# Two hybrid decoder layers in one kernel: FFN gate summed beside the output projection and closed as rows, upward product's last operand split one product sooner, closing work of the FFN spread out

## Chip, core, metric

One core of one Trainium2 chip. The metric is device time in microseconds (us); lower is better. The kernel before took 1864.57 us, the median of 3 runs (1862.85 to 1871.15).

## What is computed

Two layers over x of 1024 positions and 1024 channels, float32. Cut to what matters here:

```python
mod = silu(c) @ ada_w[l] + ada_b[l]                 # 6 rows of 1024: shift, scale, gate, twice
h = rms_norm(x, g_pre_mix[l]) * (1 + scale_m) + shift_m
q, k, v, u = split(h @ w_in[l] + b_in[l])           # 512, 128, 128, 512 columns
mix = concat([sliding_window_attention(q, k, v), causal_pool_mixer(u)]) @ w_out[l]
x = x + gate_m * rms_norm(mix, g_post_mix[l])
h = rms_norm(x, g_pre_ffn[l]) * (1 + scale_f) + shift_f
f = (silu(h @ w_gate[l]) * (h @ w_up[l])) @ w_down[l]     # 2816 channels between
x = x + gate_f * rms_norm(f, g_post_ffn[l])
```

The last `gate_f` is what this page calls the FFN gate: a row of 1024 numbers, made from the vector c and a 1024 x 1024 block of ada_w alone.

## The kernel before

Every large product is made of three matmuls in a rounded format: each operand is split into a rounded part `hi` and a remainder `lo` (`split`, L221: ScalarE rounds at L223, VectorE subtracts at L224), and hi·hi + hi·lo + lo·hi are summed in a PSUM bank (`mm3`; `mm` issues at L286). There are four `acc` banks, three `msc` banks and one `pv` bank, each 128 x 512. The sequence is worked on in two halves of 512 positions, four tiles of 128 each.

A layer goes through these stages:

1. Input projection, attention and pooling of both halves, and the output projection of each half (`mix_out`, `natural_proj`). On TensorE the order is written out by hand: `weave` runs a main stream and takes steps of side chains (attention, pooling, sums for the modulation) as soon as enough matmul columns have been issued. The unit of their gaps is `STEP`, twelve matmuls of 512 columns. `LEADS`, `GAPS`, `CLOSE` and the numbers in the calls are such gaps.
2. The upward product (w_gate and w_up together), by a seven-product scheme (Strassen-like) over 2 x 2 blocks. `up_firsts` makes the two products that need only the first half; `up_pair` makes the other five for each of 11 pairs of channel blocks. A product is two banks of four steps of three matmuls, so 24 matmuls.
3. The downward product (`down`), by the same scheme: p1, p2, p5, p6, p3, p7, p4, each over 11 pairs.

Outside the hand-written part the order of instructions on an engine is set when the program is built; engines run their own queue strictly in that order. SyncE ("SP") issues nearly all DMAs in the same way.

In `up_pair` (L1350) two `raw` buffers of 128 x 2048 hold a pair's weights: `raws[0]` has a11 and a21, `raws[1]` has a12 and a22. There are only two such buffers, so the next pair's loads (L1358) wait until the last split or sum has read the old ones. The products are, in order, T2 (a21+a22-a11, sums L1390 and L1391), T3 (a22-a11, L1396), T1 (a21+a22), B22 (a12 less the first sum, L1395) and T4 (a22 itself). `times` splits a product's left operand into `hi` and `lo`, of which there are three tiles of 1024 each, and multiplies. `added` evicts a bank with VectorE (L1375). `gated` applies silu on ScalarE (L1300) and multiplies on VectorE (L1301). L1409, L1411, L1413 and L1420 form sums that the downward product needs; `keep` stores (L1378).

The modulation rows are summed on VectorE: `ada_sum` and `ada_flow` multiply the eight 128 x 512 pieces of a block by a number per partition and accumulate (L367 and L369 in the one, L611 and L613 in the other). The sum over partitions is then a matmul with ones. `ada_gate_columns` closes a gate with four 128x1 products a half (L562), and turns the columns into rows with a transpose (L575); `ada_gate` closes it with two products whose result is one row of 512 columns (L543, L544). The FFN gate is summed by `ada_stream` during the upward product and closed as columns. The next layer's rows are summed during the downward product of layer 0 (42 steps asked of them in 77).

In `natural_proj` the last step k evicts: for each of four banks three matmuls, a square sum on ScalarE, and a multiplication by G on VectorE (L850). The second half of the columns needs the same banks again. `post_ffn` and `finish` add the residual (L769, L770); `ended` does what follows a closed bank in `down` (evictions L1470).

Of the kernel before, what the change touches and what calls it, by code (L numbers as in the profile page):

```python
# [12 lines left out]
F32R = mybir.dt.float32r  # L13
# [55 lines left out]
def hybrid_decoder_kernel(  # L69
# [556 lines left out]
    CLOSE = 1.35  # L626
# [145 lines left out]
    def post_ffn(h, fn, ss, G, into=None):  # L772
# [3 lines left out]
        sq = t_("rs", [P, 8])  # L776
        for t in range(NT):
# [7 lines left out]
            nc.sync.dma_start(new[rows, :], fn[t])  # L785
            yield
        spill[h] = new
        normalise(fn, inv_rms(sq), into)
        yield
# [31 lines left out]
    def natural_proj(fn, left, wsrc, ss, G, last, free):  # L821
# [7 lines left out]
        for nh in range(2):  # L829
# [3 lines left out]
            for k in range(K):  # L833
# [7 lines left out]
                else:  # L841
# [3 lines left out]
                    split(lh, ll, left[k])  # L845
                for t in range(NT):
                    mm3(banks[t], lh[:, tiles[t]], ll[:, tiles[t]], wh, wl, k == 0, k == K - 1)
                    if k == K - 1:
                        square_sum(ss, t, nh, banks[t])
                        nc.vector.tensor_mul(fn[t][:, cs], banks[t], G[:, cs])  # L850
                    yield
# [316 lines left out]
    LEADS = (0.9, 0.9, 0.25, 2.72, 1.2, 0.64)  # L1168
# [181 lines left out]
    def up_pair(l, p, ops, kept, xs):  # L1350
# [55 lines left out]
        bank = times(a12, B22)  # L1406
        added(X, bank, X)
# [8 lines left out]
        bank = times(a22, T4)  # L1416
# [24 lines left out]
    def left_of(a, p0, p1, c0, c1):  # L1441

        n, w = p1 - p0, c1 - c0
        raw, lh, ll = (
            part(tag, 2 * w).rearrange("p (i n) -> p i n", n=w)[:, :n, :] for tag in ("raw", "hi", "lo")
        )
        nc.sync.dma_start(raw, a[:, p0:p1, c0:c1])
        split(lh, ll, raw)
        return lh, ll
# [8 lines left out]
    def down(l, wd, load, kept, fn, ended, last, prelude):  # L1458
# [91 lines left out]
        for ts in ((0, 1), (2, 3)) if last else (range(NT),):  # L1550
            banks = {t: acc_bank() for t in ts}
            final = []
            for g, (p0, p1) in enumerate(DOWN_GROUPS):
                n = p1 - p0
                lh, ll = left_of(kept[a], p0, p1, ts[0] * P, (ts[-1] + 1) * P)
# [103 lines left out]
    FIRST = (3, NPAIR - 3)  # L1659
    for l in range(DEPTH):  # L1660
# [29 lines left out]
        def gate_flow():  # L1690
            if l:
                return
            one, two = ada_gate(l, 0)
            yield from ada_flow([one], [cats[0][1][:, i, :] for i in range(4)], 2.99)
            while 1 not in cats:
                yield 0.5
            yield from ada_flow([two], [cats[1][1][:, i, :] for i in range(4)], 2.12)
# [19 lines left out]
        pair = Chain(ada_flow(ada_pair(l, 1, par["cols"], par["abf"]), ring, 0.91))  # L1717
# [6 lines left out]
        def first_half():  # L1724
            for _ in post_norm(0, fn, ss, res0):
                yield 0.58
# [36 lines left out]
        weave(dense1(), att, pair, pre, pool)  # L1763
# [3 lines left out]
        weave(out1, att)  # L1767
# [3 lines left out]
        def second_norm():  # L1771
            yield from post_norm(1, fn, ss, xs)
            region("up")
# [8 lines left out]

        norm = second_norm()
        run(firsts[1], 16 * FIRST[1], (norm, NT + 2 + HK + 2))
        drain(norm)

        nxt, jobs = None, []
        if l + 1 < DEPTH:
            nxt = layer_cols(l + 1)
# [3 lines left out]
        wd, load = down_loads(l)  # L1793

        def ups():
            for p in range(NPAIR):
                for i, _ in enumerate(up_pair(l, p, ops, kept, firsts_x if p < sum(FIRST) else None)):
# [3 lines left out]
                    yield  # L1801

        run(ups(), 5 * NPAIR + 2 * (NPAIR - sum(FIRST)), (side, 2 * ADA + 4))
        drain(side)
        G = load_gate(l, 1)
        side = ada_stream(jobs)
# [6 lines left out]
        tail, aheads, ready = [], [], []  # L1813

        def ended(name, t):
# [22 lines left out]
        def between():  # L1838
# [10 lines left out]
            yield from post_ffn(0, fn[0], ss[0], G)  # L1849
# [6 lines left out]
            (between(), 7 * NPAIR), (side, 42),  # L1856
        )
        if nxt:
            region("mix")
            xs1 = wide_tiles("cfb")  # L1860
            drain(post_ffn(1, fn[1], ss[1], G, xs1))
# [37 lines left out]
```

## Time and profile before

| | |
|---|---|
| median of 3 runs | 1864.57 us |
| profiled execution | 1868.22 us |
| its span, first to last instruction | 1866.5 us |
| mean granted clock of TensorE | 0.996 |
| first matmul starts | 12 us after the span's start |
| output projection of the second half | about 286 to 330 us, and 1205 to 1249 us |
| upward product, five products a pair | about 418 to 732 us, and 1337 to 1648 us |

Of a row of the profile: the engine (PE is TensorE's matmuls, PEld its weight loads, DVE is VectorE, ACT is ScalarE, SP is SyncE), the line of the kernel, the operation, what it writes and reads (`lo<-raw,hi`), shape and type, and how many. In a timeline the first two numbers are start and length in us, and brackets hold the engine's idle time before it and who ended it. Matmuls overlap: a matmul of 512 columns is shown with 0.39 us, but in a dense row they start 0.227 us apart.

### The profile page before, as it was taken

Reading aid. Unit: us, or ns where it says so; the run is one execution under the profiler, and the core shown is the slowest. Engines: PE = TensorE matmul, PEld = TensorE weight load, DVE = VectorE, ACT = ScalarE, POOL = GpSimd, SP = SyncE. Lnnn points to the kernel's source line nnn. Section 1 sums busy time; section 2 is a strip of 40 time slices with the busy share of each in tenths; the row PEclk is TensorE's granted clock in tenths of the full one; section 3 lists DMA queues with packets and bytes.
Section 4 is the critical chain, followed back from the end, with each engine's and each line's share of the span. In section 5 each row is a group of like instructions: output and inputs, shape, how many; then the busy total and the mean of one; then the engine's idle time right before and its main releaser. Section 6 shows DMA issues by size and latency. Waiting matters only on the chain.

```text
span 1866.5 us, 25197 instructions
## 1 busy us (share of the span) xinstructions
PE 1826.6 (98%) x8641; PEld 1509.6 (81%) x8641; DVE 1493.2 (80%) x2468; ACT 928.1 (50%) x1770; POOL 75.3 (4%) x144
## 2 busy tenths in 40 slices
PE   7999999999999999999999999999999999999998
PEld 5887888888788788888888878888887887888886
DVE  7799885688878878799967798856888887877687
ACT  4885895562222223454657758856522222244452
POOL 0022110000000000000001201100000000000000
PEclk9999999999999999999999999999999999999999
DMA  9637654665555465955577475546646555574343
GB/s 323 233 118 231 241 167 142 215 216 174 170 182 186 173 223 188 318 187 177 196 254 240 147 237 212 172 145 214 217 151 204 176 191 204 190 267 142 116 141 119
DMA packets 237166, 363.84 MB, mean 195 GB/s; under 512 B 17951, under 2 KB 126439, under 8 KB 237037
## 3 DMA queue, kind: packets, MB, share of 16 engines
q1 hardware_dynamic: 236428, 360.12, 57.6%
q10 hardware_dynamic: 576, 2.10, 0.3%
q8 instruction: 68, 1.11, 0.2%
q14 instruction: 62, 0.50, 0.1%
q0 software_dynamic: 32, 0.00, 0.0%
HBM read 274.58 MB, written 87.57 MB: 194 GB/s over the span
## 4 chain that ended last, share of the span: by engine, by line
PE 69%; DVE 15%; DMA 7%; ACT 5%; issue 3%; SPq 1%; DVEq 0%; ACTq 0%; POOL 0%; POOLq 0%
PE acc L286 63%; DVE lo L224 3%; PE msc L286 3%; PE msc L291 2%; DMA raw<-in_w_up_dram 2%; DMA raw<-in_w_gate_dram 1%; DMA ar<-x 1%; DVE fn L1375 1%; ACT hi L223 1%; PE pv L286 1%; DVE ada L613 1%; ACT sb L1076 1%; DVE raw L1390 1%; DVE raw L1391 1%; DVE fn L1301 1%
## 5 line engine op out<-in xcount | busy, mean ns | idle before, releaser
L223 ACT ACTIVATE hi<-raw 128x1024 fp32r<-128x1024 f32 (+2 forms) x360 | 315.2, 887 | 371.5 <-PE acc L286 238.6
L224 DVE TENSOR_TENSOR lo<-raw,hi 128x1024 fp32r<-128x1024 f32 (+2 forms) x360 | 362.6, 1013 | 111.9 <-ACT hi L223 111.3
L286 PE MATMUL acc<-t,hi 128*128 128x512 f32 x1408 | 437.8, 393 | 7.9 <-ACT hi L223 7.9
L286 PEld LDWEIGHTS acc<-t,hi 128*128 128x128 f32 x1408 | 265.8, 189 | 65.0 <-ACT hi L223 9.9
L286 PE MATMUL acc<-hT,hi 128*128 128x512 f32 x928 | 287.2, 395 | 0.0
L286 PE MATMUL acc<-t,lo 128*128 128x512 f32 x704 | 275.1, 392 | 0.4 <-DVE lo L224 0.3
L286 PE MATMUL acc<-bh,hi 128*128 128x512 f32 x520 | 203.1, 391 | 0.6 <-DVE sb L1470 0.6
L286 PE MATMUL acc<-bh,lo 128*128 128x512 f32 x520 | 202.5, 390 | 0.0
L286 PEld LDWEIGHTS acc<-hT,hi 128*128 128x128 f32 x928 | 168.6, 188 | 31.1
L286 PE MATMUL acc<-hT,lo 128*128 128x512 f32 x512 | 188.1, 391 | 0.0
L1375 DVE TENSOR_TENSOR fn<-acc,fn 128x512 f32<-128x512 f32 x220 | 150.3, 684 | 36.8 <-PE acc L286 36.3
L286 PEld LDWEIGHTS acc<-t,lo 128*128 128x128 f32 x704 | 133.0, 189 | 30.0 <-DVE lo L224 1.7
L286 PE MATMUL acc<-ph,hi 128*128 128x512 f32 x328 | 126.6, 390 | 0.0
L1300 ACT ACTIVATE fn<-fn 128x512 f32<-128x512 f32 x44 | 27.9, 633 | 196.2 <-DVE fn L1375 196.2
L286 PEld LDWEIGHTS acc<-bh,hi 128*128 128x128 f32 x520 | 97.6, 188 | 21.3 <-DVE sb L1470 1.1
L286 PEld LDWEIGHTS acc<-bh,lo 128*128 128x128 f32 x520 | 97.6, 188 | 20.4
L286 PEld LDWEIGHTS acc<-hT,lo 128*128 128x128 f32 x512 | 95.5, 188 | 20.4
L286 PE MATMUL acc<-hi,hT 128*128 128x512 f32 (+1 forms) x416 | 109.1, 349 | 1.4 <-ACT hT L223 0.7
L286 PE MATMUL acc<-b,hi 128*128 128x512 f32 x352 | 108.3, 389 | 0.0
L223 ACT ACTIVATE bh<-two_b 128x512 fp32r<-128x512 f32 x100 | 62.3, 623 | 72.0 <-PE acc L286 66.7
L286 PE MATMUL acc<-hi 128*128 128x512 f32 x224 | 88.3, 394 | 2.5 <-DVE fn L850 2.4
L286 PE MATMUL acc<-lo,hi 128*128 128x512 f32 x224 | 87.3, 390 | 0.0
(327 smaller groups left out, 3171.4 us busy)
## 6 DMA issues: line engine op xcount, KB each, us to landing
raw<-in_w_gate_dram SPq DMA_DIRECT2D x44, 512.0 KB, 3.9
raw<-in_w_up_dram SPq DMA_DIRECT2D x44, 512.0 KB, 5.4
ar<-in_ada_w_dram SPq DMA_DIRECT2D x80, 256.0 KB, 3.5
raw<-keeps SPq DMA_DIRECT2D x40, 512.0 KB, 4.6
cfb<-in_ada_w_dram SPq DMA_DIRECT2D x72, 256.0 KB, 3.2
keeps<-fn SPq DMA_DIRECT2D x66, 256.0 KB, 2.1
two_b<-in_w_down_dram SPq DMA_DIRECT2D x30, 512.0 KB, 5.8
raw<-in_w_in_dram SPq DMA_DIRECT2D x52, 256.0 KB, 4.2
```

The source lines that it names most:

```text
L223: a = nc.scalar.activation(hi, src, AF.Copy)
L224: v = nc.vector.tensor_sub(lo, src, hi.bitcast(F32))
L286: return nc.tensor.matmul(dst, lhs, rhs, start=start, stop=stop)
L291: return nc.tensor.transpose(dst, src, eye_)
L613: ins = nc.vector.scalar_tensor_tensor(acc, w, c_, acc, op0=ALU.mult, op1=ALU.add)
L1076: nc.scalar.activation(S[:, i, :], S[:, i, :], AF.Exp, bias=nm[:, i : i + 1], accum_out=sm[:, i : i + 1])
L1300: nc.scalar.activation(g, g, AF.Silu)
L1301: nc.vector.tensor_mul(dst, g, u)
L1375: nc.vector.tensor_add(halves_of(dst)[m], bank, halves_of(src)[m])
L1390: nc.vector.tensor_add(a21, a21, a22)
L1391: nc.vector.tensor_sub(a11, a21, a11)
```

## The change

- The FFN gate of both layers is summed by `ada_flow` beside the second half's output projection, with two `ar` tiles as its ring (gap 1.9 STEP), and closed as rows by `ada_gate`. During layer 0's upward product the next layer's rows are summed instead, one step (two accumulations) a pair at the fourth product; during layer 1's, nothing. In the downward product 27 steps are asked instead of 42.
- `up_pair` splits a22 into two `hT` tiles of its own (`mine`), in the program text one product sooner.
- `natural_proj` holds its last step but one back and runs the last two steps bank by bank.
- The next layer's columns are read right after the second half's norm instead of after the upward product's first part.
- `post_ffn` takes two steps of the stream for one, and stores of the second half are put off. `gate_right`, the scaling by G at the end of p7 in layer 1, is put off by 4, 6, 14 and 16 steps. In the last product of layer 1 the second pass's first two left operands get `bh` tiles.
- Gaps: CLOSE 1.35 to 1.59, the second of LEADS 0.9 to 0.85, the gate's flow 2.99 to 2.54 and 2.12 to 2.11, the pair's 0.91 to 0.86, `first_half` 0.58 to 0.61.

```diff
+            if into:
+                held.append([t + 1, nc.sync.dma_start, new[rows, :], fn[t]])
...
+    held = held + [(k, lh, ll, wh, wl)] if k > K - 2 else [(k, lh, ll, wh, wl)]
+    if k == K - 2:
+        continue
     for t in range(NT):
-        mm3(banks[t], lh[:, tiles[t]], ll[:, tiles[t]], wh, wl, k == 0, k == K - 1)
-        if k == K - 1:
-            square_sum(ss, t, nh, banks[t])
-            nc.vector.tensor_mul(fn[t][:, cs], banks[t], G[:, cs])
-        yield
+        for kk, lh, ll, wh, wl in held:
+            mm3(banks[t], lh[:, tiles[t]], ll[:, tiles[t]], wh, wl, kk == 0, kk == K - 1)
+            if kk == K - 1:
+                square_sum(ss, t, nh, banks[t])
+                nc.vector.tensor_mul(fn[t][:, cs], banks[t], G[:, cs])
+            yield
...
+        def parted(src, hi, lo):
+            split(*(d.rearrange("p (a b) -> p a b", b=P) for d in (hi, lo)), src)
+            return hi, lo
         def times(src, right):
-            hi, lo = part("hi", 1024), part("lo", 1024)
-            split(*(d.rearrange("p (a b) -> p a b", b=P) for d in (hi, lo)), src)
-            return double(hi, lo, ops[right])
+            return double(*parted(src, part("hi", 1024), part("lo", 1024)), ops[right])
...
         bank = times(a12, B22)
+        parted(a22, *mine)
...
-        bank = times(a22, T4)
+        bank = double(*mine, ops[T4])
...
+        def ffn_gate():
+            yield from ada_flow(ada_gate(l, 1), [t_("ar", [P, 512]) for _ in range(2)], GATE_GAP)
...
-        weave(out1, att)
+        turn_.due = issued[0] + GATE_BEGIN * STEP
+        weave(out1, att, turn_)
+        finish_off(turn_)
...
-        side = ada_stream(ada_gate_columns(l, 1, par["cols"]))
+        side = ada_stream(jobs)
...
+                    if i == SUM_STEP and p < NPAIR - 1:
+                        next(side, None)
-        run(ups(), 5 * NPAIR + 2 * (NPAIR - sum(FIRST)), (side, 2 * ADA + 4))
+        run(ups())
...
-                    nc.vector.tensor_mul(ready[t][:, 512:D], fn[1][t][:, 512:D], G[:, 512:D])
+                    pending.append([4 + 2 * t + 6 * (t // 2), gate_right, t])
```

Lines below the edits have other numbers after the change: L1301 is L1312, L1375 is L1388, L1390 is L1403, L1391 is L1404, L1395 is L1408, L1396 is L1409, L1409 is L1423, L1411 is L1425, L1413 is L1427, L1420 is L1434, and L850 is L861.

VectorE in the upward product of layer 1, from the remainder of a pair's first left operand (`lo`) on. Before, at a pair with two steps of the gate (`ada`):

```order
L224 TENSOR_TENSOR lo<-raw,hi 128x1024
L1301 TENSOR_TENSOR fn<-fn 128x512
L1375 TENSOR_TENSOR fn<-acc,fn 128x512
L1409 TENSOR_TENSOR sb<-fn,sb 128x512
L369 SCALAR_TENSOR_TENSOR ada<-ar,c_act,ada 128x512
L1411 TENSOR_TENSOR fn<-sb,sa 128x512
L1413 TENSOR_TENSOR fn<-sa,fn 128x512
L1375 TENSOR_TENSOR fn<-acc,fn 128x512
L369 SCALAR_TENSOR_TENSOR ada<-ar,c_act,ada 128x512
L1301 TENSOR_TENSOR fn<-fn 128x512
L1396 TENSOR_TENSOR raw<-raw 128x8x128
```

The same place now:

```order
L224 TENSOR_TENSOR lo<-raw,hi 128x1024
L1409 TENSOR_TENSOR raw<-raw 128x8x128
L1388 TENSOR_TENSOR fn<-acc,fn 128x512
L1312 TENSOR_TENSOR fn<-fn 128x512
L224 TENSOR_TENSOR lo<-raw,hi 128x1024
L1423 TENSOR_TENSOR sb<-fn,sb 128x512
L1388 TENSOR_TENSOR fn<-acc,fn 128x512
L1425 TENSOR_TENSOR fn<-sb,sa 128x512
L1427 TENSOR_TENSOR fn<-sa,fn 128x512
```

The sum for the second product (L1396, now L1409) stood behind nine other instructions; now it follows the first split directly, and no `ada` stands there.

VectorE a little further on in the same pair, before. The third `lo` from the top on belongs to a22; `sb` is evicted from the third product, and L1390 is the next pair's first sum:

```order
L1375 TENSOR_TENSOR fn<-acc,fn 128x512
L224 TENSOR_TENSOR lo<-raw,hi 128x1024 x2
L1375 TENSOR_TENSOR fn<-acc,fn 128x512 x2
L224 TENSOR_TENSOR lo<-raw,hi 128x1024
L1375 TENSOR_TENSOR sb<-acc,fn 128x512
L1375 TENSOR_TENSOR fn<-acc,fn 128x512
L1375 TENSOR_TENSOR sb<-acc,fn 128x512
L1375 TENSOR_TENSOR fn<-acc,fn 128x512
L1301 TENSOR_TENSOR sb<-sb 128x512
L1390 TENSOR_TENSOR raw<-raw 128x8x128
```

And now, with a22's remainder in `hT`:

```order
L224 TENSOR_TENSOR hT<-raw,hT 128x1024
L1434 TENSOR_TENSOR fn<-fn 128x512
L1388 TENSOR_TENSOR fn<-acc,fn 128x512 x2
L224 TENSOR_TENSOR lo<-raw,hi 128x1024
L1388 TENSOR_TENSOR fn<-acc,fn 128x512 x2
L1403 TENSOR_TENSOR raw<-raw 128x8x128
L1388 TENSOR_TENSOR sb<-acc,fn 128x512
L1388 TENSOR_TENSOR fn<-acc,fn 128x512
L1404 TENSOR_TENSOR raw<-raw 128x8x128
L1408 TENSOR_TENSOR raw<-raw 128x8x128
L1388 TENSOR_TENSOR sb<-acc,fn 128x512
```

Both remainders from the second buffer (`hT` for a22, `lo` for a12) now stand ahead of the second product's evictions, where a22's stood behind them. The next pair's sums have moved up between the evictions of the third product.

TensorE at the end of the output projection of the second half, layer 0 (`hi` and `lo` are its operands, `hT` those of the first upward products), before:

```order
L286 MATMUL acc<-hi 128x512
L286 MATMUL acc<-lo,hi 128x512
L286 MATMUL acc<-hi,lo 128x512
L286 MATMUL acc<-hT,hi 128x512 x2
L286 MATMUL acc<-hT,lo 128x512
```

And now, with the added rows of the gate:

```order
L286 MATMUL acc<-hi 128x512
L286 MATMUL acc<-lo,hi 128x512
L286 MATMUL acc<-hi,lo 128x512
L543 MATMUL msc<-ph,picks 1x512
L544 MATMUL msc<-ph,picks 1x512
L286 MATMUL acc<-hT,hi 128x512 x2
```

The gate's second closing stands behind the projection's last matmul and ahead of the first upward product; its first closing stands 24 matmuls earlier, in front of the projection's last two steps.

More of the change, by code (lines that the diff above doesn't have):

```diff
@@ L784, in post_ffn @@
                 square_sum(sq, t, i, fn[t][:, cs])
-            nc.sync.dma_start(new[rows, :], fn[t])
+            if into:
+                held.append([t + 1, nc.sync.dma_start, new[rows, :], fn[t]])
+            else:
+                nc.sync.dma_start(new[rows, :], fn[t])
             yield
@@ L1439, in down_loads, with left_of @@
         return wd, load
-    def left_of(a, p0, p1, c0, c1):
+    def left_of(a, p0, p1, c0, c1, tag=None):
         n, w = p1 - p0, c1 - c0
-        raw, lh, ll = (
-            part(tag, 2 * w).rearrange("p (i n) -> p i n", n=w)[:, :n, :] for tag in ("raw", "hi", "lo")
-        )
+        wide = [part("raw", 2 * w)] + ([t_(tag, [P, 512], F32R) for _ in range(2)] if tag else [part("hi", 2 * w), part("lo", 2 * w)])
+        raw, lh, ll = (v.rearrange("p (i n) -> p i n", n=w)[:, :n, :] for v in wide)
         nc.sync.dma_start(raw, a[:, p0:p1, c0:c1])
@@ L1554, in down @@
                 n = p1 - p0
[L1555 removed]
+                lh, ll = left_of(kept[a], p0, p1, ts[0] * P, (ts[-1] + 1) * P, "bh" if ts[0] and g < 2 else None)
                 if len(kept4) == g:
@@ L1693, in gate_flow @@
             one, two = ada_gate(l, 0)
-            yield from ada_flow([one], [cats[0][1][:, i, :] for i in range(4)], 2.99)
+            yield from ada_flow([one], [cats[0][1][:, i, :] for i in range(4)], 2.54)
             while 1 not in cats:
                 yield 0.5
-            yield from ada_flow([two], [cats[1][1][:, i, :] for i in range(4)], 2.12)
+            yield from ada_flow([two], [cats[1][1][:, i, :] for i in range(4)], 2.11)
         gate = Chain(gate_flow())
@@ L1716, in hybrid_decoder_kernel @@
         ring = [cats[1][1][:, i, :] for i in range(4)]
-        pair = Chain(ada_flow(ada_pair(l, 1, par["cols"], par["abf"]), ring, 0.91))
+        pair = Chain(ada_flow(ada_pair(l, 1, par["cols"], par["abf"]), ring, 0.86))
         weave(out0, late, att, pair)
@@ L1785, in hybrid_decoder_kernel @@
         drain(norm)
-        nxt, jobs = None, []
-        if l + 1 < DEPTH:
-            nxt = layer_cols(l + 1)
+        nxt = after_[0] if after_ else None
+        jobs = []
+        if nxt:
             jobs = ada_columns(l + 1, 0, nxt["cols"], nxt["abm"]) + ada_gate_columns(l + 1, 0, nxt["cols"])
-        side = ada_stream(ada_gate_columns(l, 1, par["cols"]))
+        side = ada_stream(jobs)
         wd, load = down_loads(l)
+        mine = [t_("hT", [P, 1024], F32R) for _ in range(2)]
         def ups():
             for p in range(NPAIR):
-                for i, _ in enumerate(up_pair(l, p, ops, kept, firsts_x if p < sum(FIRST) else None)):
+                for i, _ in enumerate(up_pair(l, p, ops, kept, firsts_x if p < sum(FIRST) else None, mine)):
                     g = p - (NPAIR - len(DOWN_GROUPS))
@@ L1813, in hybrid_decoder_kernel, with gate_right @@
         tail, aheads, ready = [], [], []
+        def gate_right(t):
+            nc.vector.tensor_mul(ready[t][:, 512:D], fn[1][t][:, 512:D], G[:, 512:D])
         def ended(name, t):
@@ L1848, in between @@
                 return
-            yield from post_ffn(0, fn[0], ss[0], G)
+            for _ in post_ffn(0, fn[0], ss[0], G):
+                yield
+                yield
             for k in range(KD):
@@ L1855, in hybrid_decoder_kernel @@
             down(l, wd, load, kept, fn, ended, not nxt, prelude), 7 * NPAIR,
-            (between(), 7 * NPAIR), (side, 42),
+            (between(), 7 * NPAIR), (side, 27 if nxt else 0),
         )
+        drain(side)
         if nxt:
@@ L1860, in hybrid_decoder_kernel @@
             xs1 = wide_tiles("cfb")
-            drain(post_ffn(1, fn[1], ss[1], G, xs1))
+            for _ in post_ffn(1, fn[1], ss[1], G, xs1):
+                pass
             par = nxt
```

21 lines of the change are left out of this document (14 added, 7 removed).

## Prediction

> **What bounds the kernel now.** I read the page first: shares of the engines, then the chain that ended last.
>
> ```profile
> span 1866.5 us, 25197 instructions
> ...
> PE 1826.6 (98%) x8641; PEld 1509.6 (81%) x8641; DVE 1493.2 (80%) x2468; ACT 928.1 (50%) x1770; POOL 75.3 (4%) x144
> ...
> PE 69%; DVE 15%; DMA 7%; ACT 5%; issue 3%; SPq 1%; DVEq 0%; ACTq 0%; POOL 0%; POOLq 0%
> ```
>
> TensorE sets the time, so an edit counts only where it changes TensorE's own work or a hole in it. The next view is the table by stretches of 25 us. Five stretches in the two upward products (one per layer) have holes; 1500:1525 of the same stage has none and is the measure.
>
> ```profile
> core 0: us, PE busy (x) PEld busy (x) DVE busy (x) ACT busy (x) POOL busy (x), PEclk, DMA share, GB/s
> 500.00:525.00 25.00, 22.19 (x84) 17.40 (x84) 20.23 (x26) 6.83 (x8) 0.00 (x0) 0.86 0.45 150
> 550.00:575.00 25.00, 24.86 (x110) 20.26 (x109) 22.11 (x29) 6.73 (x9) 0.00 (x0) 1.00 0.46 157
> 625.00:650.00 25.00, 23.54 (x104) 19.02 (x103) 20.10 (x25) 6.98 (x8) 0.00 (x0) 1.00 0.49 167
> 1425.00:1450.00 25.00, 23.36 (x102) 18.80 (x101) 20.48 (x26) 6.34 (x7) 0.00 (x0) 1.00 0.59 193
> 1500.00:1525.00 25.00, 25.00 (x112) 20.71 (x111) 22.70 (x30) 7.10 (x8) 0.00 (x0) 1.00 0.54 184
> 1525.00:1550.00 25.00, 22.77 (x94) 18.34 (x93) 19.33 (x25) 5.67 (x7) 0.00 (x0) 0.93 0.46 159
> ```
>
> A dense stretch holds 112 matmuls. The others miss 28, 2, 8, 10 and 18. In the dense chain a matmul of 512 columns takes 219.78/969 = 0.2268 us:
>
> ```profile
> 1577.83 219.78 PE acc L286 x969
> ```
>
> So 38 missing matmuls in layer 0 are 8.6 us, 28 in layer 1 are 6.4 us, and the stage loses 15.0 us. Most of it is four waits, all for ScalarE's rounding of a left operand (the timeline, idle time in brackets):
>
> ```profile
> 512.38 2.50 PE L286 MATMUL acc<-t,hi 128*128 128x512 f32 x5 [2.56 <-ACT hi L223]
> ...
> 627.26 0.50 PE L286 MATMUL acc<-t,hi 128*128 128x512 f32 x1 [1.46 <-ACT hi L223]
> ...
> 1429.77 0.50 PE L286 MATMUL acc<-t,hi 128*128 128x512 f32 x1 [1.64 <-ACT hi L223]
> ...
> 1542.21 0.50 PE L286 MATMUL acc<-t,hi 128*128 128x512 f32 x1 [2.23 <-ACT hi L223]
> ```
>
> These are 7.9 us. The rest of the 15.0 us follows them: after the two long ones the clock is granted in part.
>
> ```profile
> 510.00:515.00 5.00, 2.62 (x6) 2.14 (x7) 5.00 (x7) 2.96 (x3) 0.00 (x0) 0.68 0.79 252
> 515.00:520.00 5.00, 5.00 (x16) 3.88 (x16) 2.15 (x3) 0.00 (x0) 0.00 (x0) 0.64 0.70 232
> ```
>
> 515:520 has no hole at all and still holds 16 matmuls where 22 fit. A hole of 2.2 to 2.6 us thus costs more than itself here; those of 1.46 and 1.64 us lie in stretches with clock 1.00. (The Trainium skill, "TensorE: Matmul & The Clock Gate", the table "Why this matters for your kernels", wants a hole over about 3 us before the clock falls back. By it only the 7.9 us of holes would be lost, and the stage's term below would be about 7. The rows differ and decide.)
>
> The chain of waits up to 512.38 says who was late (start, length, what):
>
> ```profile
> 490.95 7.56 DMA raw<-in_w_up_dram
> ...
> 498.54 1.23 DVE raw L1390
> ...
> 506.29 0.07 DVE ada L369
> 506.36 0.51 issue
> ...
> 508.76 0.06 DVE ada L369
> ...
> 510.02 1.15 DVE raw L1396
> ...
> 511.27 1.06 ACT hi L223
> ```
>
> The next pair's weights land at 498.5, VectorE forms the sum L1390 and then has no pause for 12.5 us; ahead of L1396, which ScalarE needs, stand evictions and two accumulations of the gate, 0.58 us each on this path. The chains to the other three waits have the same form, L369 twice included. Two things are late: the weights and VectorE's queue. The table of waits shows the first:
>
> ```profile
> DVE raw L1390 <- DMA raw<-in_w_up_dram: 15.9, 9, 3.7
> ...
> DVE raw L1390 <- issue: 13.5, 8, 2.8
> ...
> SPq L1358 <- DVE lo L224: 91.7, 43, 6.6
> ```
>
> VectorE stood at L1390 in 17 pairs for 29.4 us, 1.7 us each; the loads had themselves waited for VectorE's split, the last reader of the weights' buffer.
>
> **The change, part by part.** The sum is made against the profiled execution, 1868.22 us (span 1866.5 us); the median of the runs shown, 1864.57 us, is 3.65 us below, and the same difference is taken off it.
>
> *Upward product.* Two edits act. First, the operand a22 is split into tiles of its own, which no other product holds. Both second-half operands are then split by the end of the pair's first product instead of its second: the next pair's second weights start one product, 24 x 0.2268 = 5.4 us, sooner. L1403 (L1390 before) has also moved forward, from behind the third product's evictions to between its two halves, half a product or 2.7 us. That leaves 2.7 us more room against a wait of 1.7 us. L1409 (L1396 before), which was last in the queue above, now stands directly behind the first split, ahead of the gate's product. Second, the FFN gate's 16 accumulations leave the stage: in layer 1 nothing replaces them, in layer 0 as many of the next layer's stand there, at a fixed product of each pair. Both causes of the four waits go, in layer 1 twice over. I keep a tenth for what stays: 15.0 x 0.9 = -13.5 us. Bounds: -15.0 (all holes) and +26 (the second rival at its longest wait); -6.4 if only layer 1 is cured. What is late next is VectorE: 22.70 of 25 us in the dense stretch, 2.5 us free in a pair of 27.2 us.
>
> *TensorE's own work.* The gate was closed by one-column products, now by rows:
>
> ```profile
> L562 PE MATMUL msc<-ones_r,ada 128*128 128x1 f32 x48 | 5.7, 239 | 0.0
> ```
>
> Of three such gates two go: 32 instructions of 5.7/48 = 0.12 us, 3.8 us. Eight row products of 512 columns come, 8 x 0.2268 = 1.8 us. Net -2.0 us, from 0 (the small ones hidden) to -2.3 us (two transposes go too).
>
> *Gate beside the second output projection.* Its 16 accumulations a layer cost 16 x 0.745 = 11.9 us of VectorE, and it has the room:
>
> ```profile
> L613 DVE SCALAR_TENSOR_TENSOR ada<-cfb,c_act,ada 128x512 f32<-128x512 f32 x63 | 46.9, 745 | 1.0 <-DMA cfb<-in_ada_w_dram 0.6
> ```
>
> ```profile
> 286.00:330.00 44.00, 44.00 (x196) 36.43 (x195) 20.57 (x32) 21.74 (x40) 0.00 (x0) 1.00 0.47 150
> ```
>
> 23.4 us of 44 are idle there, so this costs nothing; without that cover it would be 11.9 us a layer. But its two closings stand in TensorE's queue and wait for their split; behind them stands the whole projection, or the first upward product. The nearest row is a closing of the other gate:
>
> ```profile
> 115.03 0.40 PE L543 MATMUL msc<-ph,picks 128*1 128x512 f32 x1 [0.57 <-DVE pth L224]
> ```
>
> Four closings, 0 to 0.6 us each; I take +1.0 us, since both splits stand ahead of an eviction in VectorE's queue. The loads wait on SyncE for a ring of two buffers, and the projection's weights stand behind them; those are several steps ahead. The next layer's columns, now read during the first upward products, add seven small loads and one transpose there: 0, as the order leaves three products of 5.4 us between the last of these loads and the transpose.
>
> *Output projection, last two steps together.* Each accumulator now closes two steps apart. It bears on the second half of columns, which waits for its banks:
>
> ```profile
> 175.73 0.50 PE L286 MATMUL acc<-hi 128*128 128x512 f32 x1 [1.40 <-DVE fn L850]
> ...
> 178.75 0.50 PE L286 MATMUL acc<-hi 128*128 128x512 f32 x1 [0.30 <-DVE fn L850]
> ...
> 1095.52 0.50 PE L286 MATMUL acc<-hi 128*128 128x512 f32 x1 [0.73 <-DVE fn L850]
> ```
>
> The first bank closes 2.0 us sooner, which covers each wait alone, but VectorE still has one to four other instructions between two evictions. Of 2.4 us I take -1.3; bounds 0 and -2.4.
>
> *Closing work spread out, operands of the last product in other tiles.* It aims at two waits:
>
> ```profile
> 858.37 0.50 PE L286 MATMUL acc<-bh,hi 128*128 128x512 f32 x1 [0.65 <-DVE sb L1470]
> ...
> 1829.46 0.50 PE L286 MATMUL acc<-one_b,hi 128*128 128x512 f32 x1 [0.58 <-DVE sa L1470]
> ```
>
> In layer 0 a third of the accumulations leaves the downward product; in layer 1 the scaling of ready rows is put off. -0.8 us of 1.2; bounds 0 and -1.2. The tail behind the last matmul is untouched. The stores put off in layer 0 leave SyncE's queue freer and are waited for only a layer later: 0.
>
> *Leads and gaps in the attention part.* They only shift small pieces among TensorE's matmuls.
>
> ```profile
> PE msc L291 <- DVE pth L224: 2.8, 2, 1.4
> ```
>
> These and the closing above are 3.4 us that can go, and a shift may as well make two new waits of 1.4 us: -0.4, from -3.4 to +2.8.
>
> Sum: -13.5 - 2.0 + 1.0 - 1.3 - 0.8 - 0.4 = -17.0 us. 1868.2 - 17.0 = 1851.2 us for an execution like the profiled one; **1864.6 - 17.0 = 1847.6 us** for the median.
>
> **Rivals.** *Layer 0 keeps its holes.* There the accumulations stay, only paced otherwise, and VectorE remains the fuller. For it: two L369 in each chain. Against it: the order puts L1409 ahead of them. Then 8.6 x 0.9 = 7.7 us do not come: 1847.6 + 7.7 = 1855.3 us, within 0.5%.
>
> *VectorE stands at L1403.* It is now queued ahead of the second half of the third product's evictions; if the weights are late, those banks stay full. The stage has 2.5 us free in a pair; a wait of w costs w - 2.5 in each of 22 pairs. At 3.3 us that is 17.6 us, and the 13.5 do not come: 1847.6 + 31.1 = 1878.7 us; at the longest wait seen, 3.7 us, 1887.5 us. It costs from 2.5 us a pair and makes the kernel slower by over 0.5% (1873.9 us) from 3.1 us. Against it: 1.7 us is the mean now, and the load gains 2.7 us.
>
> *The change does not reach the holes.* They were placed by the drift of VectorE against TensorE, and may form at other pairs at half the price: 1847.6 + 6.8 = 1854.4 us, with new waits at the closings (2.3 us, 1.3 more than taken) 1855.7 us.
>
> **How the numbers follow.** A measurement of this kernel tells about 0.5%, 9.3 us, from no change: faster means below 1855.2 us. My forecast has 0.72, layer 0's rival 0.13, holes at other places 0.09, VectorE at L1403 0.06. The forecast's own range is 1842 (all waits named gone: -15.0 - 2.3 - 2.4 - 1.2 - 3.4 + 0 = -24.3 would be 1840.3, not all at once) to 1853 (half of layer 0's holes and the closings' full wait). With the two middle rivals it reaches 1858. Faster: 0.72, 0.04 of layer 0's rival and 0.02 of the third, 0.78; slower: the rival at L1403, 0.06; the rest, 0.16, within.
>
> **What would show it.** Right: the stretches of the upward product hold 112 matmuls at clock 1.00 in both layers; L1403's wait for the weights is near nothing; no 128x1 group of 48 but of 16. Layer 0's rival: holes there alone, with L369 in their chain. L1403: VectorE's wait for raw above 2.5 us a pair, followed by TensorE's for an eviction. The forecast is wrong if the stage is dense and the time still above 1855 us: then the new closings or the reordered attention took it.

## The result, and the profile after

The changed kernel takes **1849.97 us** (median of 5 runs, 1847.82 to 1850.42), beside 1862.85 us for the kernel before in 5 runs on the same chip (1860.70 to 1871.15): ratio 0.992, 95% interval 0.9896 to 0.9943. The forecast was 1847.6 us, 17.0 us less than before. Between these medians the gain is 12.9 us; where the changed kernel was timed again (series B and C below) it is 17.8 and 12.7 us. The profiled execution took 1850.02 us, 18.2 us less than the one of before (1868.22 us, itself above its median); the table of stages compares these two executions, so its sum lies at the upper end of what the medians show.

The page of the changed kernel, head, engines and the chain that ended last:

```profile
span 1848.3 us, 25196 instructions
...
PE 1816.4 (98%) x8615; PEld 1504.5 (81%) x8615; DVE 1497.9 (81%) x2472; ACT 929.3 (50%) x1772; POOL 71.6 (4%) x144
...
PE 70%; DVE 16%; ACT 5%; DMA 5%; issue 4%; SPq 0%; DVEq 0%; ACTq 0%; POOL 0%; POOLq 0%
```

TensorE still sets the time. To see where the 18.2 us come from I cut both executions at the same places of the program: the last transpose of the second half's norm (`msc<-ident,fn`, behind the output projection) and the first eviction of the downward product. Between them lies the upward product, with the start of the downward one up to its first closed bank. Before, layer 0 and layer 1 (the first two numbers are the stretch and its length):

```profile
400.52:790.76 390.24, 385.83 (x1701) 317.53 (x1700) 316.80 (x417) 116.02 (x146) 0.00 (x0) 0.99 0.60 204
...
1319.72:1705.12 385.40, 381.53 (x1683) 314.85 (x1682) 305.87 (x394) 116.10 (x146) 0.00 (x0) 1.00 0.58 199
```

And the changed kernel, with two stretches of 25 us besides:

```profile
400.41:785.16 384.75, 381.78 (x1690) 314.31 (x1689) 312.00 (x409) 114.22 (x145) 0.00 (x0) 1.00 0.59 205
...
1311.08:1688.14 377.06, 377.06 (x1666) 312.17 (x1665) 293.90 (x374) 115.20 (x145) 0.00 (x0) 1.00 0.56 191
575.00:600.00 25.00, 23.35 (x106) 18.79 (x105) 21.45 (x30) 6.99 (x8) 0.00 (x0) 1.00 0.44 152
500.00:525.00 25.00, 25.00 (x112) 20.67 (x112) 20.46 (x27) 5.81 (x7) 0.00 (x0) 1.00 0.59 200
```

In layer 1 TensorE is busy for all of 377.06 us: the stage is dense. In layer 0 it is busy for 381.78 of 384.75 us, and 575:600 holds 106 matmuls where 500:525 holds 112. All stages, in us, with the prediction's terms put to their stages (the output projection's and the closing work's by the size of their waits, leads and gaps in halves; of the 32 one-column products, counted net, 8 went in layer 0's upward product, 8 in its downward product and 16 in layer 1's upward product):

| stage | before | after | change | forecast |
|---|---|---|---|---|
| layer 0 up to the end of the output projection | 400.5 | 400.4 | -0.1 | +0.3 |
| layer 0, upward product | 390.2 | 384.7 | -5.5 | -8.7 |
| layer 0, downward product to its last products | 135.8 | 134.0 | -1.8 | -1.4 |
| layer 1 up to the end of the output projection | 393.1 | 391.9 | -1.3 | +0.8 |
| layer 1, upward product | 385.4 | 377.1 | -8.3 | -7.7 |
| layer 1, downward product | 154.1 | 153.0 | -1.1 | -0.4 |
| sum, with the tail (-0.1) | | | -18.2 | -17.0 |

The sum came out between these two executions, with errors that cancel; layer 0 did not. What TensorE waits for there has changed. The timeline of the changed kernel, TensorE (start, length, idle time in brackets):

```profile
580.78 3.02 PE L286 MATMUL acc<-t,hT 128*128 128x512 f32 x12 [1.08 <-DVE fn L1388]
584.38 2.79 PE L286 MATMUL acc<-t,hT 128*128 128x512 f32 x11 [0.57 <-DVE fn L1388]
```

Before, TensorE waited for a rounded operand (ScalarE, L223). Now the operand is there, and the bank is not free: it waits for an eviction. What VectorE does ahead of the first of these:

```profile
569.37 1.21 DVE L224 TENSOR_TENSOR lo<-raw,hi 128x1024 fp32r<-128x1024 f32 x1
570.50 1.28 DVE L1388 TENSOR_TENSOR fn<-acc,fn 128x512 f32<-128x512 f32 x2
578.31 1.23 DVE L1403 TENSOR_TENSOR raw<-raw 128x1024 f32<-128x1024 f32 x1 [6.53 <-DMA raw<-in_w_up_dram]
579.45 0.68 DVE L1388 TENSOR_TENSOR sb<-acc,fn 128x512 f32<-128x512 f32 x1
580.05 0.68 DVE L1388 TENSOR_TENSOR fn<-acc,fn 128x512 f32<-128x512 f32 x1
```

VectorE stands at L1403, the next pair's first sum, for 6.53 us. The evictions behind it (`sb`, the third product's) can't begin, and TensorE resumes when they are done. The chain of waits says why the weights come so late: the load is issued only when the last split of the old weights has ended at 570.6 us, and takes 7.14 us:

```profile
569.44 1.14 DVE lo L224
...
570.60 0.38 SPq L1369
...
571.04 7.14 DMA raw<-in_w_up_dram
```

This is no single event. Groups by line, VectorE in the changed kernel (behind the second bar the idle time ahead of the group, and who ended it):

```profile
L1388 DVE TENSOR_TENSOR fn<-acc,fn 128x512 f32<-128x512 f32 x220 | 148.6, 682 | 22.0 <-PE acc L286 21.9
L1388 DVE TENSOR_TENSOR sb<-acc,fn 128x512 f32<-128x512 f32 x44 | 30.1, 684 | 4.7 <-PE acc L286 4.7
L1403 DVE TENSOR_TENSOR raw<-raw 128x1024 f32<-128x1024 f32 x22 | 27.0, 1225 | 90.0 <-DMA raw<-in_w_up_dram 74.2 <-DMA fn<-firsts 13.6 <-DMA keepa<-sb 2.1
```

The same three groups before:

```profile
L1375 DVE TENSOR_TENSOR fn<-acc,fn 128x512 f32<-128x512 f32 x220 | 150.3, 684 | 36.8 <-PE acc L286 36.3
L1375 DVE TENSOR_TENSOR sb<-acc,fn 128x512 f32<-128x512 f32 x44 | 30.4, 691 | 42.6 <-PE acc L286 42.5
L1390 DVE TENSOR_TENSOR raw<-raw 128x1024 f32<-128x1024 f32 x22 | 27.0, 1226 | 37.0 <-DMA raw<-in_w_up_dram 15.9 <-issue 13.5 <-DMA sa<-keepa 4.5
```

Read the three together: 116.4 us idle before, 116.7 us now. VectorE's idle time at these three is what it was; it has moved from the evictions, where VectorE waited for TensorE, to L1403, where TensorE may wait for VectorE. That L1403's wait grew from 1.7 to 4.1 us a pair (90.0/22) was the mark of the prediction's worst rival, and yet the kernel is faster.

### The profile page after: what moved, and what is told of

It is laid out like the page before. It is cut to its first block, busy times and chain, and to the rows that moved or that the text cites. A ratio compares the mean times of both kernels' runs of the same rounds, so it can differ in the third digit from the quotient of the medians.

```text
span 1848.3 us, 25196 instructions
## 1 busy us (share of the span) xinstructions
PE 1816.4 (98%) x8615; PEld 1504.5 (81%) x8615; DVE 1497.9 (81%) x2472; ACT 929.3 (50%) x1772; POOL 71.6 (4%) x144
## 4 chain that ended last, share of the span: by engine, by line
PE 70%; DVE 16%; ACT 5%; DMA 5%; issue 4%; SPq 0%; DVEq 0%; ACTq 0%; POOL 0%; POOLq 0%
PE acc L286 63%; PE msc L286 3%; DVE lo L224 2%; DMA raw<-in_w_up_dram 2%; DVE fn L1388 2%; PE msc L291 2%; PE pv L286 1%; DMA fn<-firsts 1%; DVE ada L613 1%; ACT sb L1087 1%; ACT junk L660 1%; DVE hT L224 1%; DVE raw L1408 1%; DVE fn L1312 1%; ACT hi L223 1%
## 5 line engine op out<-in xcount | busy, mean ns | idle before, releaser
L223 ACT ACTIVATE hi<-raw 128x1024 fp32r<-128x1024 f32 (+1 forms) x336 | 291.7, 879 | 306.3 <-PE acc L286 169.6
L224 DVE TENSOR_TENSOR lo<-raw,hi 128x1024 fp32r<-128x1024 f32 (+1 forms) x336 | 334.9, 1000 | 79.1 <-ACT hi L223 78.1
L286 PE MATMUL acc<-t,hi 128*128 128x512 f32 x1056 | 325.3, 389 | 0.0
L286 PEld LDWEIGHTS acc<-t,hi 128*128 128x128 f32 x1056 | 198.0, 188 | 41.5 <-issue 0.3
L286 PE MATMUL acc<-t,lo 128*128 128x512 f32 x528 | 205.4, 389 | 0.0
L1388 DVE TENSOR_TENSOR fn<-acc,fn 128x512 f32<-128x512 f32 x220 | 148.6, 682 | 22.0 <-PE acc L286 21.9
L1311 ACT ACTIVATE sb<-sb 128x512 f32<-128x512 f32 x38 | 24.0, 632 | 253.3 <-DVE sb L1388 228.9
L286 PE MATMUL acc<-t,hT 128*128 128x512 f32 x528 | 124.8, 391 | 3.0 <-DVE fn L1388 3.0
L286 PEld LDWEIGHTS acc<-t,hT 128*128 128x128 f32 x528 | 98.6, 188 | 25.7 <-DVE fn L1388 5.3
L286 PEld LDWEIGHTS acc<-t,lo 128*128 128x128 f32 x528 | 99.1, 188 | 20.5
L1403 DVE TENSOR_TENSOR raw<-raw 128x1024 f32<-128x1024 f32 x22 | 27.0, 1225 | 90.0 <-DMA raw<-in_w_up_dram 74.2
```

The costliest lines, as they stand in the source:

```text
L223: a = nc.scalar.activation(hi, src, AF.Copy)
L224: v = nc.vector.tensor_sub(lo, src, hi.bitcast(F32))
L286: return nc.tensor.matmul(dst, lhs, rhs, start=start, stop=stop)
L1311: nc.scalar.activation(g, g, AF.Silu)
L1388: nc.vector.tensor_add(halves_of(dst)[m], bank, halves_of(src)[m])
L1403: nc.vector.tensor_add(a21, a21, a22)
```

## The experiments

Times are medians; each ratio is to the kernel before in the same series, with its 95% interval. The series stand in the table by the kernel before: A 1868.26 us, B 1867.77 us, C 1866.28 us. The lengths of the two upward products are cut as above, each from one profiled execution. Three of these are the longest of their runs: before with own tiles (1867.18 us), sums at the old pace (1855.01 us) and the projection's last step as before (1862.44 us).

| run | series | us | ratio | layer 0 | layer 1 |
|---|---|---|---|---|---|
| before |  | 1862.85 | 1 | 390.2 | 385.4 |
| changed, first |  | 1849.97 | 0.9920 (0.9896 to 0.9943) | 384.7 | 377.1 |
| changed, second | B | 1850.01 | 0.9907 (0.9893 to 0.9920) | 385.2 | 377.8 |
| changed, third | C | 1853.61 | 0.9927 (0.9912 to 0.9943) | 386.7 | 378.3 |
| a22 in shared tiles | A | 1847.60 | 0.9896 (0.9879 to 0.9913) | 380.5 | 378.4 |
| before, a22 in own tiles | A | 1862.38 | 0.9971 (0.9960 to 0.9982) | 386.4 | 381.9 |
| no sums in layer 0's stage | A | 1855.24 | 0.9932 (0.9920 to 0.9945) | 380.2 | 381.4 |
| sums at the old pace, shared tiles | B | 1851.58 | 0.9917 (0.9902 to 0.9931) | 387.4 | 378.8 |
| L1403 behind evictions | A | 1845.09 | 0.9878 (0.9864 to 0.9892) | 379.9 | 377.1 |
| the same again | C | 1845.42 | 0.9881 (0.9865 to 0.9898) | 379.9 | 377.1 |
| the same, shared tiles | C | 1847.93 | 0.9898 (0.9882 to 0.9914) | 382.0 | 378.6 |
| projection's last step as before | B | 1857.17 | 0.9945 (0.9930 to 0.9959) | 386.8 | 380.4 |
| gaps as before | B | 1853.27 | 0.9925 (0.9912 to 0.9939) | 386.4 | 377.1 |
| closing work as before | C | 1854.28 | 0.9934 (0.9918 to 0.9949) | 384.9 | 378.6 |

The theory on trial is the prediction's: the four holes go because a22 has tiles of its own and the next weights start sooner. The rivals are that the gate's sums did it, by leaving the stage or by their new place, and that VectorE's standing at L1403 costs what is left.

### Own tiles or sums

The changed kernel with a22 split into the shared `hi` and `lo` again, everything else kept:

```diff
-        parted(a22, *mine)
...
-        bank = double(*mine, ops[T4])
+        bank = times(a22, T4)
```

> The changed kernel, but a22 is split as before, from the shared hi and lo tiles; the gate stays out of the upward product. Theory A (the split in tiles of its own, hence earlier loads, cures the upward product): without it holes for a rounded operand come back in both layers, about 9 us more than the changed kernel's 1850, so 1857 to 1860 us. Theory B (the gate's accumulations were the cause): layer 1 stays dense, layer 0 loses 5 to 9 us, 1850 to 1854 us.

1847.60 us. Its upward products:

```profile
400.82:781.29 380.47, 380.26 (x1690) 314.74 (x1689) 314.55 (x409) 116.34 (x145) 0.00 (x0) 1.00 0.61 207
1306.83:1685.26 378.43, 377.41 (x1666) 312.01 (x1665) 296.05 (x375) 116.09 (x145) 0.00 (x0) 1.00 0.56 191
```

Without own tiles both stages are nearly dense, layer 0 far more so than in the changed kernel, and the kernel is no slower. Its timeline, VectorE in layer 1:

```profile
1536.27 0.69 DVE L1388 TENSOR_TENSOR sb<-acc,fn 128x512 f32<-128x512 f32 x1 [1.43 <-PE acc L286]
...
1537.48 0.68 DVE L1312 TENSOR_TENSOR sb<-sb 128x512 f32<-128x512 f32 x1
1538.49 1.23 DVE L1403 TENSOR_TENSOR raw<-raw 128x1024 f32<-128x1024 f32 x1 [0.33 <-DMA raw<-in_w_up_dram]
```

L1403 stands behind the third product's evictions here, as before, and waits for 20.9 us in all where it waits for 90.0 in the changed kernel. It is with the own tiles that the order built from the program has it ahead of them. The opposite, the kernel before with only the own tiles added:

```diff
+        parted(a22, *mine)
...
-        bank = times(a22, T4)
+        bank = double(*mine, ops[T4])
```

> The kernel before with a22's tiles of its own and nothing else; the gate stays in the upward product. Theory A: the holes shrink in both layers from 15 us to about 5 each at most in sum, 1852 to 1856 us. Theory B: the gate's accumulations still hold up the queue, the holes stay, 1860 to 1864 us.

1862.38 us, 5.9 us less than the kernel before in its series; in the profile the upward products are 3.8 and 3.5 us shorter than before (386.4 and 381.9), and holes stay in both. So the own tiles alone bring something, but they are neither needed nor enough: the theory falls as the main cause. Moving the sums away, which the prediction had as its second reason, cures the stage without the first.

This run also shows what that one edit does to the next pair's first sum (L1392 here). The order now has it between or ahead of the third product's evictions, and VectorE waits there for 77.2 us, where it waited 37.0 us before:

```profile
L1392 DVE TENSOR_TENSOR raw<-raw 128x1024 f32<-128x1024 f32 x22 | 27.0, 1225 | 77.2 <-DMA raw<-in_w_up_dram 55.4 <-issue 7.1 <-DMA fn<-firsts 6.8
```

### Whether the sums cost by their number or by their place

Layer 0's upward product without any sum; all 42 steps are asked of them in the downward product, as before:

```diff
-                    if i == SUM_STEP and p < NPAIR - 1:
-                        next(side, None)
...
-            (between(), 7 * NPAIR), (side, 27 if nxt else 0),
+            (between(), 7 * NPAIR), (side, 42 if nxt else 0),
```

> The changed kernel without any accumulation in layer 0's upward product; all of the next layer's are made in its downward product (42 steps asked, as before). If layer 0's remaining 4.9 us of holes come from VectorE's load, they go and some tenths come back in the downward product: 1845 to 1847 us, no eviction wait in 560 to 700 us. If they come from the place of the next pair's first sum alone, they stay: 1849 to 1851 us.

1855.24 us, slower than either expectation. Layer 0's upward product takes 380.2 us, as good as dense, although VectorE still stands at L1403 for 4.0 us a pair there (44.1 us over 11). So in layer 0 the changed kernel's holes need both, the sums and the early L1403. The downward product behind it takes 138.5 us where the changed kernel has 134.0: what the one stage gains, 4.5 us, the other loses. Layer 1's takes 381.4 us here although VectorE's order in it is that of the changed kernel, with four waits of 0.5 to 0.6 us for evictions: with L1403 ahead of evictions the same code came out between 377.1 and 381.4 us in seven profiles. What picks one or the other is not settled.

The same number of sums in layer 0 at the old pace, by columns of TensorE instead of at a fixed product, with shared tiles (the partner is therefore the first experiment):

```diff
-                    if i == SUM_STEP and p < NPAIR - 1:
-                        next(side, None)
...
-        run(ups())
+        run(ups(), 5 * NPAIR + 2 * (NPAIR - sum(FIRST)), (itertools.islice(side, 2 * ADA), 2 * ADA + 4))
```

> The run without tiles of a22's own, and layer 0's ten steps of sums spread over the products at the old pace instead of one a pair at the fourth product; their number is the same and layer 1 has none. If their place makes the holes (two accumulations ahead of the sum for the second product), layer 0 loses 5 to 9 us again: 5 to 9 us above that run, ratio to the kernel before 0.992 to 0.995. If only their number counts, nothing changes: ratio 0.989 to 0.991.

1851.58 us, ratio 0.9917 against 0.9896: less than the 5 to 9 us expected, and the two intervals overlap. In the profile layer 0 takes 387.4 us against 380.5 with the fixed place, layer 1, where the two do not differ, 378.8 against 378.4. Both make 16 accumulations among layer 0's pairs, but here TensorE waits for a left operand again, 1.40, 0.45 and 2.55 us, and with the fixed place it does not. In these two traces it is the place of the sums in VectorE's queue that makes such holes, not their number; what the place is worth in the medians these runs do not fix.

### The place of L1403

The changed kernel with one constraint: the next pair's first sum comes behind the third product's last eviction.

```diff
-        nc.vector.tensor_add(a21, a21, a22)
+        first = nc.vector.tensor_add(a21, a21, a22)
+        if "third" in recent:
+            after(first, recent.pop("third"))
...
         added(E, bank, U)
         added(X, bank, X)
+        recent["third"] = recent["evicted"]
```

> The changed kernel with the next pair's first sum held behind the third product's evictions, as it stood before. If the wait for the weights in front of those evictions makes layer 0's 4.9 us of holes, they go: 1845 to 1847 us, and VectorE's wait at that sum falls from 4.2 us a pair to about 1. If VectorE's load makes them, they stay or turn into waits for ScalarE's rounding: 1849 to 1853 us.

1845.09 us, the fastest version. Groups by line:

```profile
L1388 DVE TENSOR_TENSOR fn<-acc,fn 128x512 f32<-128x512 f32 x220 | 150.4, 683 | 28.5 <-PE acc L286 28.2
L1388 DVE TENSOR_TENSOR sb<-acc,fn 128x512 f32<-128x512 f32 x44 | 30.4, 692 | 74.9 <-PE acc L286 74.9
L1403 DVE TENSOR_TENSOR raw<-raw 128x1024 f32<-128x1024 f32 x22 | 26.8, 1219 | 3.7 <-DMA keepa<-sb 2.1 <-DMA raw<-in_w_up_dram 1.6
```

```profile
399.07:778.99 379.92, 379.92 (x1690) 314.84 (x1689) 314.15 (x409) 115.34 (x145) 0.00 (x0) 1.00 0.61 208
1304.42:1681.48 377.06, 377.06 (x1666) 312.16 (x1665) 294.13 (x375) 115.34 (x145) 0.00 (x0) 1.00 0.56 191
```

The wait at L1403 is gone (3.7 us in all for 90.0), VectorE's idle time lies at the evictions again, where it harms nobody, and both stages are dense. It was timed again with the changed kernel beside it, and with a22 in shared tiles as well:

> The changed kernel, unaltered, as the common measure of the runs beside it. Both theories: 1850.0 us, as in its two timings so far (1849.97 and 1850.01), TensorE's waits in the upward product of layer 0 again for evictions (L1388), 4 to 5.5 us in all, and layer 1 nearly dense.

> The changed kernel with the next pair's first sum (L1403) placed behind all evictions of the third product, beside the changed kernel on one chip. If VectorE standing at L1403 ahead of evictions is what leaves layer 0's holes, it is 4 to 6 us faster than the changed kernel here too (about 1845 us), and both upward products stay dense. If its first timing (1845.09) was the luck of one chip, the two are within 1.5 us of each other.

> Both remedies at once: a22 in the shared tiles again, and L1403 placed behind the third product's evictions. With the shared tiles alone VectorE waited 18 us at L1403 and the kernel took 1847.6 us. If the place of L1403 is what counts, the time is that of the pinned kernel with a22's own tiles, 1845 us within 1.5 us. If a22's own tiles help as well once the standing is out of the way, it is 2 us or more above that kernel, with waits for hi (L223) back in the upward products.

The changed kernel took 1853.61 us (1850.52 to 1857.41), more than the 1850.0 expected, the constrained one 1845.42 us (1843.20 to 1846.57): 8.2 us less, with no run in common. With shared tiles it is 1847.93 us, 2.5 us more with no run in common, though the intervals of the two ratios overlap, and waits for `hi` and `lo` are back (0.45 us at 562.8 us, 1.03 us at 564.6 us). By its ratio (0.9898) it is the first experiment (0.9896), where the sum stood behind these evictions without a constraint. The own tiles thus seem of use once L1403 stands where it should; with L1403 too early (0.9907 to 0.9927) they seem to lose more than they give.

### Output projection, gaps, closing work

Three more parts were undone one at a time. First the changed kernel again, as their measure; then the projection's last step, the gaps and the closing work:

> The changed kernel once more, beside the variants on one chip: ratio to the kernel before 0.990 to 0.994. If holes in front of the third product's evictions depend on when loads happen to land, their places and sum in the upward product differ from the first profile's 4.9 us in layer 0 and none in layer 1, by several us; if they are set by the program alone, they are the same.

```diff
-                held = held + [(k, lh, ll, wh, wl)] if k > K - 2 else [(k, lh, ll, wh, wl)]
-                if k == K - 2:
-                    continue
+                held = [(k, lh, ll, wh, wl)]
```

> The changed kernel with the output projection's last step as before. By the prediction the banks' waits come back: 1 to 2 us above the changed kernel, with waits for an eviction of 1 to 1.5 us near 175 us and of 0.7 us in layer 1. Rival: what delayed those evictions was the modulation's sums in VectorE's queue, whose gap has also changed, and no more than 0.5 us comes back.

```diff
-    CLOSE = 1.59
+    CLOSE = 1.35
...
-                yield 0.61
+                yield 0.58
```

> The changed kernel with all gaps and leads of the attention part as before (CLOSE, LEADS, the gate's, the pair's, the half's). By the prediction 0.4 us slower, within -2.8 and +3.4. The profile after shows no less lost in 75 to 275 us than before (7.6 us against 7.2), so the rival is that the new gaps bring nothing: 0 to 1.5 us faster.

```diff
-            if into:
-                held.append([t + 1, nc.sync.dma_start, new[rows, :], fn[t]])
...
-                    pending.append([4 + 2 * t + 6 * (t // 2), gate_right, t])
+                    gate_right(t)
```

> The changed kernel with the closing work as before: post_ffn's doubled steps, the put-off stores, the put-off gate_right and the bh tiles of the last product undone. By the prediction's term it is 0.8 us slower than the changed kernel (0 to 1.2), and the waits at about 843 us for sb (L1483) and 1815 us for sa come back with 0.6 us each. The rival: the output projection's last step and the gaps each cost more when undone than the waits that they had removed (7 and 3 us for 1.3 and 0.4), so a part undone shifts the work behind it; then this one costs 2 to 4 us too, with new holes elsewhere.

*Changed kernel again*: 1850.01 us, ratio 0.9907. TensorE's waits for evictions at L1388 are 3.1 us in 6 (4.7 us in 8 in the third profile) against 3.0 us in 5 in the first, with one near 581, 584, 669 and 696 us in all three: the places are largely the program's, the lengths vary. *Projection*: 1857.17 us against 1850.01, with intervals that do not meet. The two parts up to the end of the projections are 2.6 and 3.0 us longer than in the second profile of the changed kernel (403.2 and 395.0). TensorE's waits for L859, the eviction there, come to 2.2 us in 4, against 0.7 us in 2 in the first profile of the changed kernel; the longest lies at 312 us in the second half's projection, where before had none and where the gate's accumulations now run beside it. A further 1.9 us is a wait for `rs` (L352) at 973 us, which the changed kernel has with 1.3 us or less. The rest is not accounted for. *Gaps*: 1853.27 us against 1850.01; the intervals overlap, and between nothing and 7 us all remains possible. In the traces the new gaps take away a wait of 1.34 us at 84.6 us (for `pth`) and bring one of 1.04 us at 111.6 us (for `ar`, L545). *Closing work*: 1854.28 us against 1853.61, no difference that the runs can tell. In its profile the last downward product takes 154.3 us against 153.0 to 153.1 in the three profiles of the changed kernel, with the wait for `sa` back (0.76 us at 1813.8 us); layer 0's takes 134.1 us, as in the changed kernel. The projection's expected 1.3 us was too little by several us; the closing work's rival, new holes elsewhere, did not come.

## Why the prediction held, and where it did not

The total of 17.0 us stands beside 18.2 us between the two executions and 12.7 to 17.8 us between medians. That it came this near is in part luck: one term fell short, others gave more than was summed.

*Upward product, -13.5 us, with the one-column products that leave it (24 x 0.12 us) -16.4.* Measured -13.8, which leaves -10.9 for the waits: layer 1 as forecast, layer 0 short, and the first reason not the cause. The step that failed reads: "L1403 (L1390 before) has also moved forward, from behind the third product's evictions to between its two halves, half a product or 2.7 us. That leaves 2.7 us more room against a wait of 1.7 us." The rows of the order, quoted with the change, show L1403 ahead of the first `sb`, that is ahead of all the third product's evictions, and VectorE arrives at an instruction when the one ahead of it ends: here behind the second product's evictions, a whole product sooner and not half (so in 16 of the 20 pairs after the first of each layer; in four it does stand between the halves). And the split came sooner by less than a product. Before, at a pair of layer 1:

```profile
1491.94 1.22 DVE L224 TENSOR_TENSOR lo<-raw,hi 128x1024 fp32r<-128x1024 f32 x1 [0.18 <-ACT hi L223]
1493.79 0.69 DVE L1375 TENSOR_TENSOR sb<-acc,fn 128x512 f32<-128x512 f32 x1 [0.63 <-PE acc L286]
...
1497.71 0.68 DVE L1301 TENSOR_TENSOR sb<-sb 128x512 f32<-128x512 f32 x1
1500.36 1.23 DVE L1390 TENSOR_TENSOR raw<-raw 128x1024 f32<-128x1024 f32 x1 [1.97 <-issue]
```

And with the constraint, own tiles kept:

```profile
1470.59 1.22 DVE L224 TENSOR_TENSOR hT<-raw,hT 128x1024 fp32r<-128x1024 f32 x1
...
1475.42 0.69 DVE L1388 TENSOR_TENSOR sb<-acc,fn 128x512 f32<-128x512 f32 x1 [2.03 <-PE acc L286]
...
1479.35 0.68 DVE L1312 TENSOR_TENSOR sb<-sb 128x512 f32<-128x512 f32 x1
1479.95 1.22 DVE L1403 TENSOR_TENSOR raw<-raw 128x1024 f32<-128x1024 f32 x1
```

The last split starts 1.9 us ahead of the first `sb` in the one and 4.8 us in the other. From its end to VectorE's arrival at the sum there are 5.2 us before (1493.16 to 1498.39), 8.1 us with the constraint, and 1.2 us in the changed kernel (570.58 to 571.78, quoted above). The last two are among the shortest of their kind. Over the same 20 pairs the split starts 1.7 us ahead of the first `sb` on average before and 6.0 us with the constraint: 4.3 us sooner by the own tiles, where 5.4 were counted. From its end to VectorE's arrival there are 5.1 us on average before, 9.4 with the constraint, and 2.7 (1.2 to 4.0) in the changed kernel. So the changed kernel did not gain 2.7 us of room; it lost 2.4.

*The rival at L1403* had its mechanism right and its price wrong. It put the free time of VectorE at 2.5 us a pair, from one stretch of 25 us, shorter than a pair. Ten whole periods of each layer, from the first L1403 to the eleventh, in the constrained kernel, which is dense:

```profile
412.68:684.35 271.67, 271.67 (x1204) 225.07 (x1203) 228.48 (x292) 70.73 (x82) 0.00 (x0) 1.00 0.56 189
1318.58:1588.74 270.16, 270.16 (x1193) 223.72 (x1192) 217.28 (x274) 70.44 (x81) 0.00 (x0) 1.00 0.51 175
```

VectorE is free for 4.3 us a pair in layer 0, where the sums stand, and for 5.3 us in layer 1, where none do. The changed kernel's waits at L1403 are 4.3 us a pair in layer 0 (up to 6.5) and 3.9 in layer 1 (up to 5.4): they take all of the room in the one, with holes, and fit into that of the other, which is dense in the first profile.

*Layer 0 keeps its holes* is what happened in small: 384.7 us where 379.9 is dense, 4.8 us of the 7.7 that the rival gave up, but by evictions behind L1403 and not by accumulations ahead of L1409, though without accumulations these holes went too. The layer's -5.5 us therefore fell 3.2 us short.

*TensorE's own work*, the group of small closings:

```profile
L562 PE MATMUL msc<-ones_r,ada 128*128 128x1 f32 x16 | 1.9, 239 | 0.0
```

It holds 16 where it held 48, as said. *The new closings* (+1.0) cost nothing: TensorE waits at none of their four places (about 324, 330, 1235 and 1241 us). *Output projection* (-1.3): the waits that it aimed at went from 2.4 to 0.7 us; undone it costs 5.6 us in its own stages, in the longest execution of that run. What the rest of it is stays open, and so does why layer 1's first part gained 1.3 us where +0.8 was summed; the closings explain 0.5 us of that. *Closing work* (-0.8): near 1.2 us by the profiles, all in layer 1; the medians do not show it. *Leads and gaps* (-0.4): not told apart from nothing. Between the two executions, layer 0's shortfall of 3.2 us was made up by 2.1 us in layer 1's first part, 0.6 us in its upward product and 0.7 us in its downward product, and some tenths elsewhere.

## What to carry to other kernels

An instruction that waits for a transfer should stand in an in-order queue behind the evictions that TensorE will need during that transfer: count its arrival from the end of the instruction ahead of it, not from where its neighbours used to run. An engine's free time is taken over whole periods and includes its waits for others; if it is the same after a change, ask at which instruction it now stands and who is queued behind. When a change with two remedies works, undo each alone: here the one that seemed to be the cure was holding the other back.

## What the runs showed of the hardware

The granted clock already fell behind holes of about 2 us. The changed kernel, third profile, across a hole of 1.71 us that ends at 670.33 us:

```profile
665.00:670.00 5.00, 3.62 (x16) 2.65 (x15) 3.37 (x4) 0.76 (x1) 0.00 (x0) 1.00 0.32 125
670.00:675.00 5.00, 4.67 (x21) 3.86 (x21) 5.00 (x7) 0.93 (x2) 0.00 (x0) 1.00 0.14 52
```

The sums at the old pace, across one of 2.55 us that ends at 624.06 us:

```profile
620.00:625.00 5.00, 2.45 (x11) 1.60 (x9) 5.00 (x7) 2.05 (x3) 0.00 (x0) 1.00 0.91 289
625.00:630.00 5.00, 5.00 (x17) 3.93 (x16) 3.70 (x5) 0.91 (x1) 0.00 (x0) 0.66 0.52 144
630.00:635.00 5.00, 5.00 (x24) 4.14 (x23) 2.83 (x5) 1.12 (x2) 0.00 (x0) 1.00 0.70 249
```

And the projection's last step as before, across one of 1.90 us that ends at 973.29 us:

```profile
970.00:975.00 5.00, 3.10 (x15) 2.55 (x14) 4.59 (x14) 0.72 (x2) 0.00 (x0) 0.84 0.82 318
975.00:980.00 5.00, 5.00 (x37) 5.00 (x36) 2.13 (x7) 2.19 (x2) 1.00 (x4) 0.82 0.89 316
```

After 1.71 us the clock stays at 1.00. After 2.55 us it is 0.66 in the next 5 us, and 17 matmuls run where 24 follow: that hole costs another 1.6 us (7 x 0.2268). (Such a row also counts matmuls that only reach into it; the 16 of the prediction's row 515:520 stand against 24 in the same way, not against 22.) After 1.90 us it is 0.84 and 0.82. The length of one hole does not decide alone. In the kernel before with own tiles three shorter ones, each with another close by, were followed by a lower clock: 1.76 us that end at 424.88 us, with 0.55 us three us earlier (0.66 in 425:430), 1.42 us at 792.29 us, with 0.29 us a us later (0.77 in 795:800), and 1.40 us at 1008.99 us, with 0.46 us three us earlier (0.77 in 1010:1015). Single holes of 1.40 us (sums at the old pace, 510.23 us) and of 1.46 and 1.64 us (before) left it at 1.00. The Trainium skill ("TensorE: Matmul & The Clock Gate", the table "Why this matters for your kernels") names about 3 us; here single holes of 1.90 us and more already paid.
